# The low part of each weight chunk by a DMA that adds the raw chunk to its negated high part

## The chip, the cores and the metric

The kernel runs on one core of a Trainium2 chip. The metric is the device time of one execution in microseconds, as the median of the runs shown. TensorE is called PE, VectorE DVE, ScalarE ACT, GpSimd POOL and SyncE SP, as in the profile.

## What is computed

Two stacked blocks on a sequence of 512 tokens of width 1024. The first has two layers of dilated attention, an mLSTM, two gated projections and an MLP; the second has one layer with a state-space scan, top-k attention, a pooling mixer, three gated branches and a gated MLP. Almost all arithmetic is in the matrix products of the activations with float32 weights:

```python
def hybrid_layer(x, cos, sin, ...):
    h = rms_norm(x, norm_mix_w)
    z = h @ w_in + b_in
    ...
    mixed = ga * (ya @ w_proj_att) + gb * (yb @ w_proj_mlstm)
    x = x + mixed @ w_out
    h2 = rms_norm(x, norm_mlp_w)
    x = x + jnp.square(jax.nn.relu(h2 @ w_ff1)) @ w_ff2

def _layer(h, ...):
    proj = xn @ w_in
    ...
    merged = g[:, :, 0] * (y_ssd @ w_up_ssd) + g[:, :, 1] * (y_att @ w_up_attn) + g[:, :, 2] * (y_pool @ w_up_pool)
    h = h + merged @ w_out
    a_part, b_part = jnp.split(hn @ w_ffn_in, 2, axis=-1)
    return h + (jax.nn.silu(a_part) * b_part) @ w_ffn_out
```

## The kernel before, in words

**Three products for one.** PE multiplies in a float32 type with fewer mantissa bits (F32R). So each operand is split into a high part, which is the value rounded to that type, and a low part, the value minus its high part. A product of weights and activations is then high by high, high by low and low by high. In `lin` these are lines 280, 281 and 282: 280 and 281 read the high weights `wh`, and 282 reads the low weights `wl`. In `lin_tok` (319 to 321) the roles of the operands are exchanged.

**Chunks.** The weights come in chunks of 128 partitions by 1024 float32, 512 KB each, laid out on the host in the order of use. `chunk` (line 219) makes one ready. SP loads the raw chunk into `wr` (line 231). ACT copies it into `wh`, which rounds it (line 250). Then the low part `wl` is the raw chunk minus `wh`: on DVE (line 256), or in a fixed share of the chunks of some phases on POOL (line 254; the table `SHARE` sets the share). The first two chunks are made in pieces at lines 247 and 248, and the last few, with `keep`, go through `split`. `wr`, `wh` and `wl` have three buffers each, so a chunk's buffers come free when PE has done with the chunk three before it.

**The use of a chunk.** A chunk of a product over 1024 inputs holds one tile of 128 output columns and gives PE 24 matmuls. `lin_cols` (line 286) uses chunks one at a time, except for the first `lead` tiles of a call. With `lead` 2 the first two tiles are run together, each k of the one beside the same k of the other, so that both chunks must be there at nearly the same moment. I call two such chunks a pair, and a chunk that runs alone a single. By the table `LEAD` and the calls with `lead=2` there are, besides the pair that opens the program, 10 pairs in the first layer, 11 in the second (qk 1, gb 4, the output projection 1, ff1 1, ff2 4) and 25 in the second block (the gates of the branches 12, the state-space up-projection 4, the rest 9): 46 in all.

**Background work.** Attention, mLSTM, scan, indexer and pooling are generators that are advanced while the matrix products run (`tick`). All engines work their queues in order. A scheduler sets the order in each queue at build time, from its own estimates.

**The rotary embedding.** `ev_qk` (line 639) evacuates one of the eight query and key tiles, and its `turn` (lines 652 to 654) puts three operations on POOL. In the first layer these wait for `self.sin` (line 600).

```python
            h = self.wp.tile([P, CHUNK], F32R, name=self.name("wh"), tag="wh")
            nc.scalar.activation(h[:, :n], src, AF.Copy)
            nc.vector.tensor_tensor(lo[:, :n], src, h[:, :n].bitcast(F32), ALU.subtract)
```

Of the kernel before, what the change touches and what calls it, by code (L numbers as in the profile page):

```python
# [10 lines left out]
F32 = mybir.dt.float32  # L11
F32R = mybir.dt.float32r
I32 = mybir.dt.int32
AF = mybir.ActivationFunctionType
ALU = mybir.AluOpType
# [135 lines left out]
class Build:  # L151
# [67 lines left out]
    def chunk(self, key, l, rows, cs, keep=False):  # L219

        nc = self.nc
        kt, m = len(rows) // P, len(cs)
        i = self.nchunk
        self.nchunk += 1
        self.recipes.append((key, l, rows, cs))
        n = kt * m
        if i < 2:
            raw = self.raw[i]
        else:
            raw = self.wp.tile([P, CHUNK], F32, name=self.name("wr"), tag="wr")  # L230
            nc.sync.dma_start(raw[:, :n], self.dram["w"][i, :, :n])
        src = raw[:, :n]
        if keep:
            out = [], []
            for k in range(0, kt, 4):
                c = src[:, k * m : min(k + 4, kt) * m]
                for o, part in zip(out, self.split(c, n=c.shape[-1])):
                    o.extend(part[:, x * m : x * m + m] for x in range(min(4, kt - k)))
            return out
        h = self.wp.tile([P, CHUNK], F32R, name=self.name("wh"), tag="wh")  # L240
        lo = self.wp.tile([P, CHUNK], F32R, name=self.name("wl"), tag="wl")
        if i < 2:
            for a, b in FIRST:
                with ExitStack() as order:
                    for x in self.lead if a else ():
                        order.enter_context(self.tc.issue_after(x.ins))
                    nc.scalar.activation(h[:, a:b], src[:, a:b], AF.Copy)
                    nc.vector.tensor_tensor(lo[:, a:b], src[:, a:b], h[:, a:b].bitcast(F32), ALU.subtract)
            return tuple(x[:, :n].rearrange("p (k m) -> p k m", k=kt) for x in (h, lo))
        nc.scalar.activation(h[:, :n], src, AF.Copy)  # L250
        self.share += SHARE[self.phase]
        if self.share >= 1.0:
            self.share -= 1.0
            nc.gpsimd.tensor_tensor(lo[:, :n], src, h[:, :n].bitcast(F32), ALU.subtract)  # L254
        else:
            nc.vector.tensor_tensor(lo[:, :n], src, h[:, :n].bitcast(F32), ALU.subtract)  # L256
        v = lambda x: x[:, :n].rearrange("p (k m) -> p k m", k=kt)
        return v(h), v(lo)

# [1335 lines left out]
```

## Time and profile before

| | us |
|---|---|
| median of 3 runs | 2476.59 (2476.35 to 2478.15) |
| the profiled execution's own time | 2479.92 |
| its span, first to last instruction | 2478.1 |
| PE busy | 2442.3 (99%) |
| DVE busy | 1457.4 (59%) |
| ACT busy | 1005.0 (41%) |
| POOL busy | 438.7 (18%) |

The profiled execution is 3.3 us above the median. A matmul's duration in the trace overlaps the next one's, so the pace of PE is read from the distance of their starts. A wait is put down to the engine that the profile names as its releaser.

### The profile page before, as it was taken

Reading aid. Unit: us, or ns where it says so; the run is one execution under the profiler, and the core shown is the slowest. Engines: PE = TensorE matmul, PEld = TensorE weight load, DVE = VectorE, ACT = ScalarE, POOL = GpSimd, SP = SyncE. Lnnn points to the kernel's source line nnn. Section 1 sums busy time; section 2 is a strip of 40 time slices with the busy share of each in tenths; the row PEclk is TensorE's granted clock in tenths of the full one; section 3 lists DMA queues with packets and bytes.
Section 4 is the critical chain, followed back from the end, with each engine's and each line's share of the span. In section 5 each row is a group of like instructions: output and inputs, shape, how many; then the busy total and the mean of one; then the engine's idle time right before and its main releaser. Section 6 shows DMA issues by size and latency. Waiting matters only on the chain. (4 is left out here: it accounts for less than half of the span.)

```text
span 2478.1 us, 28176 instructions
## 1 busy us (share of the span) xinstructions
PE 2442.3 (99%) x10892; PEld 1950.7 (79%) x10892; DVE 1457.4 (59%) x2428; ACT 1005.0 (41%) x1483; POOL 438.7 (18%) x348
## 2 busy tenths in 40 slices
PE   9999999999999999999999999999999999999998
PEld 8777788888888877778888887777777778888887
DVE  7776655433447577655433446866898755434344
ACT  5567533332234377533332324344324633322222
POOL 4520010000311530011000120343332200101010
PEclk9999999999999999999999999999999999999999
DMA  4221223332223322223233332221222223332332
GB/s 160 90 79 54 69 85 95 102 94 94 94 94 94 98 65 77 68 77 102 86 102 96 94 99 86 77 85 52 80 84 70 77 77 94 102 94 92 96 91 71
DMA packets 63045, 216.46 MB, mean 87 GB/s; under 512 B 7232, under 2 KB 10304, under 8 KB 62912
## 3 DMA queue, kind: packets, MB, share of 16 engines
q1 hardware_dynamic: 60480, 212.14, 27.6%
q8 instruction: 85, 1.39, 0.2%
q10 hardware_dynamic: 2112, 1.48, 0.2%
q0 software_dynamic: 320, 1.05, 0.2%
q14 instruction: 48, 0.39, 0.0%
HBM read 212.55 MB, written 2.10 MB: 87 GB/s over the span
## 5 line engine op out<-in xcount | busy, mean ns | idle before, releaser
L280 PE MATMUL pb<-h,wh 128*128 128x512 f32 x2976 | 1199.8, 403 | 0.5 <-DVE tok L671 0.5
L282 PE MATMUL pb<-h,wl 128*128 128x512 f32 x2976 | 1180.8, 397 | 6.0 <-DVE wl L256 5.2
L281 PE MATMUL pb<-l,wh 128*128 128x512 f32 x2976 | 1180.5, 397 | 0.0
L250 ACT ACTIVATE wh<-wr 128x1024 fp32r<-128x1024 f32 (+1 forms) x393 | 410.6, 1054 | 959.9 <-PE pb L281 665.0
L282 PEld LDWEIGHTS pb<-h,wl 128*128 128x128 f32 x2976 | 562.9, 189 | 139.5 <-DVE wl L256 8.6
L280 PEld LDWEIGHTS pb<-h,wh 128*128 128x128 f32 x2976 | 563.0, 189 | 134.6 <-issue 8.2
L281 PEld LDWEIGHTS pb<-l,wh 128*128 128x128 f32 x2976 | 562.9, 189 | 130.0 <-issue 5.1
L256 DVE TENSOR_TENSOR wl<-wr,wh 128x1024 fp32r<-128x1024 f32 (+1 forms) x366 | 481.5, 1319 | 272.8 <-ACT wh L250 270.8
L254 POOL TENSOR_TENSOR wl<-wr,wh 128x1024 fp32r<-128x1024 f32 x27 | 67.7, 2506 | 403.2 <-ACT wh L250 362.3
L822 POOL TENSOR_TENSOR y<-y,rbc 128x512 f32<-128x512 f32 x16 | 24.7, 1542 | 561.3 <-DVE y L820 561.3
L1211 DVE TENSOR_TENSOR f<-pb,rbc 128x512 f32<-128x512 f32 x44 | 30.4, 691 | 123.9 <-PE pb L282 123.9
L1215 POOL TENSOR_TENSOR f<-f,fs 128x512 f32<-128x512 f32 x22 | 38.3, 1742 | 347.6 <-ACT fs L1214 347.6
L265 ACT ACTIVATE h<-f 128x512 fp32r<-128x512 f32 x86 | 54.4, 632 | 109.2 <-DVE f L808 88.1
L830 DVE TENSOR_TENSOR x<-x,pb 128x512 f32<-128x512 f32 x40 | 27.5, 688 | 99.3 <-PE pb L282 99.2
L266 DVE TENSOR_TENSOR l<-f,h 128x512 fp32r<-128x512 f32 x86 | 59.4, 690 | 44.8 <-ACT h L265 44.8
L525 DVE SCALAR_TENSOR_TENSOR cv<-cz,par,cv 128x512 f32<-128x512 f32 x84 | 73.0, 869 | 7.1 <-ACT cv L523 5.7
L820 DVE TENSOR_TENSOR y<-y,pb 128x512 f32<-128x512 f32 x32 | 22.0, 688 | 92.1 <-PE pb L282 92.1
L453 ACT ACTIVATE s<-s,ng 128x128 f32<-128x128 f32 (+3 forms) x96 | 53.4, 557 | 39.2 <-DVE ng L452 37.7
L319 PE MATMUL pb<-wh,h 128*128 128x512 f32 x128 | 51.0, 399 | 0.0
L320 PE MATMUL pb<-wh,l 128*128 128x512 f32 x128 | 50.7, 396 | 0.0
L735 DVE TENSOR_TENSOR gate<-pb,rbc 128x512 f32<-128x512 f32 x40 | 27.3, 687 | 39.4 <-PE pb L282 39.3
L321 PE MATMUL pb<-wl,h 128*128 128x512 f32 x128 | 50.4, 396 | 0.0
(396 smaller groups left out, 2365.5 us busy)
## 6 DMA issues: line engine op xcount, KB each, us to landing
wr<-in_w_dram SPq DMA_DIRECT2D x381, 512.0 KB, 3.6
wr<-in_w_dram SPq DMA_DIRECT2D x16, 448.0 KB, 3.3
x<-in_x_dram SPq DMA_DIRECT2D x8, 256.0 KB, 5.7
out_dram<-o SPq DMA_DIRECT2D x8, 128.0 KB, 2.4
out_dram<-o ACTq DMA_DIRECT2D x8, 128.0 KB, 2.5
wr<-in_w_dram SPq DMA_DIRECT2D x2, 384.0 KB, 5.4
bb<-in_bav_dram POOLq DMA_DIRECT2D x2, 256.0 KB, 3.9
bb<-in_bmv_dram POOLq DMA_DIRECT2D x2, 256.0 KB, 3.5
```

The lines of the kernel that those rows point to most:

```text
L250: nc.scalar.activation(h[:, :n], src, AF.Copy)
L254: nc.gpsimd.tensor_tensor(lo[:, :n], src, h[:, :n].bitcast(F32), ALU.subtract)
L256: nc.vector.tensor_tensor(lo[:, :n], src, h[:, :n].bitcast(F32), ALU.subtract)
L265: nc.scalar.activation(h[:, :n], src, AF.Copy)
L266: nc.vector.tensor_tensor(lo[:, :n], src, h[:, :n].bitcast(F32), ALU.subtract)
L280: mm(ps[:m, :], a, xh, start=k == 0, stop=False)
L281: mm(ps[:m, :], a, xl, start=False, stop=False)
L282: mm(ps[:m, :], b, xh, start=False, stop=k == n - 1)
L319: mm(ps[b], ah, wh[:, kk, :], start=k == 0, stop=False)
L320: mm(ps[b], al, wh[:, kk, :], start=False, stop=False)
L453: nc.scalar.activation(s[:, :n], s[:, :n], AF.Exp, bias=ng, scale=-1.0, accum_out=ls)
L525: nc.vector.scalar_tensor_tensor(a, z[:, 1 + j : 1 + j + T], w[:, j : j + 1], a, ALU.mult, ALU.add)
```

## The change

In the branch for chunks whose low part DVE made, two instructions take the place of the subtraction. ACT writes the raw chunk once more, negated, into `wl`; the output type rounds it, so this is the negated high part. Then POOL issues a DMA that reads the raw chunk a second time from DRAM and adds it onto `wl` in place. The branch for POOL's own subtractions stays.

```diff
         if self.share >= 1.0:
             self.share -= 1.0
             nc.gpsimd.tensor_tensor(lo[:, :n], src, h[:, :n].bitcast(F32), ALU.subtract)
         else:
-            nc.vector.tensor_tensor(lo[:, :n], src, h[:, :n].bitcast(F32), ALU.subtract)
+            nc.scalar.activation(lo[:, :n], src, AF.Copy, scale=-1.0)
+            nc.gpsimd.dma_start(lo[:, :n], self.dram["w"][i, :, :n], accum_op=ALU.add)
```

The scheduler orders every queue anew; lines below 256 have numbers one higher in the changed kernel. Three places matter for what follows.

The first is ACT's queue in the first layer, where a pair of chunks for `gb` is made while the single chunk before it runs. Before, `wh_2996` and `wh_3003` are the pair:

```order
L265 ACTIVATE h_2876<-m_638_2873 128x512
L250 ACTIVATE wh_2996<-wr_2994 128x1024
L250 ACTIVATE wh_3003<-wr_3001 128x1024
L736 ACTIVATE gate_2942<-gate_2942,par_130 128x512
L736 ACTIVATE gate_2945<-gate_2945,par_130 128x512
L265 ACTIVATE h_2971<-m_656_2968 128x512
```

Now the same pair is 3036 and 3044:

```order
L266 ACTIVATE h_2914<-m_638_2911 128x512
L250 ACTIVATE wh_3036<-wr_3034 128x1024
L256 ACTIVATE wl_3037<-wr_3034 128x1024
L737 ACTIVATE gate_2982<-gate_2982,par_130 128x512
L737 ACTIVATE gate_2985<-gate_2985,par_130 128x512
L250 ACTIVATE wh_3044<-wr_3042 128x1024
L256 ACTIVATE wl_3045<-wr_3042 128x1024
```

The two negated copies are new, and the second chunk's high part now stands behind the first chunk's negated copy and two gates.

The second is PE's queue where that pair is used (`pb_3000` and `pb_3007` before, `pb_3041` and `pb_3049` now, are the two output tiles). Before:

```order
L282 MATMUL pb_2955<-h_2762,wl_2951 128x512
L280 MATMUL pb_3000<-h_149,wh_2996 128x512
L281 MATMUL pb_3000<-l_150,wh_2996 128x512
L282 MATMUL pb_3000<-h_149,wl_2997 128x512
L280 MATMUL pb_3007<-h_149,wh_3003 128x512
L281 MATMUL pb_3007<-l_150,wh_3003 128x512
L282 MATMUL pb_3007<-h_149,wl_3004 128x512
L280 MATMUL pb_3000<-h_155,wh_2996 128x512
```

Now:

```order
L281 MATMUL pb_3041<-h_149,wh_3036 128x512
L282 MATMUL pb_3041<-l_150,wh_3036 128x512
L283 MATMUL pb_3041<-h_149,wl_3037 128x512
L281 MATMUL pb_3049<-h_149,wh_3044 128x512
L282 MATMUL pb_3049<-l_150,wh_3044 128x512
L281 MATMUL pb_3041<-h_155,wh_3036 128x512
L282 MATMUL pb_3041<-l_156,wh_3036 128x512
L283 MATMUL pb_3041<-h_155,wl_3037 128x512
L281 MATMUL pb_3041<-h_161,wh_3036 128x512
L282 MATMUL pb_3041<-l_162,wh_3036 128x512
L283 MATMUL pb_3041<-h_161,wl_3037 128x512
L283 MATMUL pb_3049<-h_149,wl_3045 128x512
```

The first low part is still needed at the third matmul of the pair, the second at the twelfth and not at the sixth.

The third is POOL's queue near the start, at the rotary embedding of the first layer (`rr` and `qk` are the tiles of `turn`). Before:

```order
L381 TENSOR_TENSOR acc_153<-acc_153,sq_202 128x512
L652 TENSOR_TENSOR rr_317<-rr_317,sin_324 128x512
L652 TENSOR_TENSOR rr_322<-rr_322,sin_324 128x512
L653 TENSOR_TENSOR qk_277<-qk_277,cos_325 128x512
L653 TENSOR_TENSOR qk_319<-qk_319,cos_325 128x512
L654 TENSOR_TENSOR qk_277<-qk_277,rr_317 128x512
L654 TENSOR_TENSOR qk_319<-qk_319,rr_322 128x512
L652 TENSOR_TENSOR rr_368<-rr_368,sin_324 128x512
L653 TENSOR_TENSOR qk_365<-qk_365,cos_325 128x512
L654 TENSOR_TENSOR qk_365<-qk_365,rr_368 128x512
```

Now (the DMAs of the chunks at index 5 and 6, `wl_457` and `wl_497`):

```order
L257 DMA wl_457<-in_w_dram 128x1024
L653 TENSOR_TENSOR rr_317<-rr_317,sin_324 128x512
L653 TENSOR_TENSOR rr_322<-rr_322,sin_324 128x512
L654 TENSOR_TENSOR qk_277<-qk_277,cos_325 128x512
L654 TENSOR_TENSOR qk_319<-qk_319,cos_325 128x512
L655 TENSOR_TENSOR qk_277<-qk_277,rr_317 128x512
L655 TENSOR_TENSOR qk_319<-qk_319,rr_322 128x512
L653 TENSOR_TENSOR rr_369<-rr_369,sin_324 128x512
L654 TENSOR_TENSOR qk_366<-qk_366,cos_325 128x512
L257 DMA wl_497<-in_w_dram 128x1024
L655 TENSOR_TENSOR qk_366<-qk_366,rr_369 128x512
```

The DMA of the chunk at index 6 now stands behind eight of these operations, and the later ones behind three or four each. POOL's queue has 366 such DMAs in all.

## Rows read from the trace of the kernel before

**Rows 1.** The page: span, then busy time, share of the span and instructions.
```profile
span 2478.1 us, 28176 instructions
PE 2442.3 (99%) x10892; PEld 1950.7 (79%) x10892; DVE 1457.4 (59%) x2428; ACT 1005.0 (41%) x1483; POOL 438.7 (18%) x348
```
**Rows 2.** Groups of instructions: busy us, mean ns of one, idle before and its releaser.
```profile
L250 ACT ACTIVATE wh<-wr 128x1024 fp32r<-128x1024 f32 (+1 forms) x393 | 410.6, 1054 | 959.9 <-PE pb L281 665.0
L256 DVE TENSOR_TENSOR wl<-wr,wh 128x1024 fp32r<-128x1024 f32 (+1 forms) x366 | 481.5, 1319 | 272.8 <-ACT wh L250 270.8
L254 POOL TENSOR_TENSOR wl<-wr,wh 128x1024 fp32r<-128x1024 f32 x27 | 67.7, 2506 | 403.2 <-ACT wh L250 362.3
```
**Rows 3.** Waits of PE and its weight loads: us in total, times, longest.
```profile
PE PT L464 <- DVE ng L452: 6.0, 3, 3.6
PE pb L282 <- DVE wl L256: 5.2, 4, 2.7
PEld pb L282 <- DVE wl L256: 8.6, 7, 3.1
```
**Rows 4.** ACT in order of time, singles of the MLP: start, duration.
```profile
499.30 1.06 ACT L250 ACTIVATE wh<-wr 128x1024 fp32r<-128x1024 f32 x1 [4.04 <-PE pb L281]
500.26 0.57 ACT L818 COPY y<-pb 128x512 f32<-128x512 f32 x1
```
**Rows 5.** PE in order of time: first use of that chunk's low part.
```profile
510.94 0.40 PE L282 MATMUL pb<-h,wl 128*128 128x512 f32 x1
```
**Rows 6.** ACT and DVE in order of time, while a pair is made ready.
```profile
335.81 2.01 ACT L250 ACTIVATE wh<-wr 128x1024 fp32r<-128x1024 f32 x2 [3.29 <-PE pb L281]
337.72 1.32 ACT L736 ACTIVATE gate<-gate,par 128x512 f32<-128x512 f32 x2
335.99 1.39 DVE L735 TENSOR_TENSOR gate<-pb,rbc 128x512 f32<-128x512 f32 x2 [2.75 <-PE pb L282]
```
**Rows 7.** PE in order of time: that pair's first matmul and first low parts.
```profile
342.07 0.39 PE L280 MATMUL pb<-h,wh 128*128 128x512 f32 x1
342.53 0.39 PE L282 MATMUL pb<-h,wl 128*128 128x512 f32 x1
343.23 0.40 PE L282 MATMUL pb<-h,wl 128*128 128x512 f32 x1
```
**Rows 8.** The page: DMA queue (packets, MB, share), then issues (KB, us to landing).
```profile
q1 hardware_dynamic: 60480, 212.14, 27.6%
wr<-in_w_dram SPq DMA_DIRECT2D x381, 512.0 KB, 3.6
bb<-in_bav_dram POOLq DMA_DIRECT2D x2, 256.0 KB, 3.9
bb<-in_bmv_dram POOLq DMA_DIRECT2D x2, 256.0 KB, 3.5
```
**Rows 9.** Groups of POOL: a DMA's issue, us and mean ns.
```profile
L667 POOL DMA_DIRECT2D bb<-in_bav_dram x2 | 1.3, 660 | 0.0
```
**Rows 10.** POOL in order of time, from the first rotary operation on.
```profile
42.29 2.67 POOL L652 TENSOR_TENSOR rr<-rr,sin 128x512 f32<-128x512 f32 x2 [20.75 <-DVE sin L600]
44.90 3.55 POOL L653 TENSOR_TENSOR qk<-qk,cos 128x512 f32<-128x512 f32 x2
48.42 3.53 POOL L654 TENSOR_TENSOR qk<-qk,rr 128x512 f32<-128x512 f32 x2
51.91 1.30 POOL L652 TENSOR_TENSOR rr<-rr,sin 128x512 f32<-128x512 f32 x1
53.16 1.31 POOL L653 TENSOR_TENSOR qk<-qk,cos 128x512 f32<-128x512 f32 x1
```
**Rows 11.** DVE in order of time: evacuation of the eighth query and key tile.
```profile
58.95 0.69 DVE L641 TENSOR_TENSOR qk<-pb,rbc 128x512 f32<-128x512 f32 x1 [2.73 <-PE pb L282]
```
**Rows 12.** PE after its longest wait; busy by stretch (PE's and PEclk matter).
```profile
120.87 0.90 PE L464 MATMUL PT<-first,s 128*128 128x128 f32 x3 [3.58 <-DVE ng L452]
120.00:125.00 5.00, 4.13 (x14) 3.56 (x15) 3.80 (x9) 2.80 (x6) 0.00 (x0) 0.50 0.02 6
```

## The prediction, made before the changed kernel ran

> **What bounds the kernel now.** I read the page's busy times first: PE is busy 2442.3 of 2478.1 us [rows 1], so only 36 us of its time are idle, and an edit that frees DVE (1457.4 us busy) cannot give more than that. Then the groups of instructions: 366 low parts are made by DVE, 1319 ns each, 27 by POOL, and ACT waits 665 us for PE before its high parts [rows 2]. So the chunks are made ahead of PE, as early as a buffer comes free. The waits say the same: PE stands for a low part only 5.2 us in 4 waits, its weight loads 8.6 us in 7 [rows 3]; the two overlap. What decides is therefore the slack: the time from a finished high part to PE's first use of the low part.
>
> For a single the high part ends at 499.30 + 1.06 = 500.36 [rows 4] and the low part is first used at 510.94 [rows 5]: 10.6 us. For a pair the high parts end at 336.87 and 337.82 [rows 6] and the low parts are first used at 342.53 and 343.23 [rows 7]: 5.7 and 5.4 us, because only one single runs between the release of the buffers and the pair. PE's matmuls start 0.23 us apart [rows 7], a chunk of 24 takes 5.57 us.
>
> **What the change does to a chunk.** Removed: 366 DVE subtractions, 481.5 us [rows 2]. PE is the bound, so this gives at most what PE still waits for DVE; apart from the low parts its longest entry is 6.0 us [rows 3]. I take 5 us off, with 0 and 14 as ends. The 27 subtractions on POOL stay.
>
> Added on ACT: 366 negated copies of the same shape as the high part, 1.05 us each [rows 2], 386 us. ACT goes from 41% to 56% and is not the bound, but the copy stands between the high part and the DMA, and in front of the next high part. Added on POOL: 366 DMA issues of about 0.66 us [rows 9], 242 us, which would bring it from 18% to 28%; each waits in order for ACT's copy and behind POOL's other work, and whatever POOL has queued behind it waits too.
>
> **The new DMA's time, L, from issue to landing.** No row shows an accumulating DMA. The raw loads took 27.6% of 16 engines for 212.14 MB [rows 8]: 0.276 x 2478.1 / 212.14 x 0.524 = 1.69 us of all 16 engines for a 512 KB chunk. POOL's own loads of 256 KB land after 3.5 and 3.9 us [rows 8]; less 0.85 us of data that leaves about 2.85 us of fixed time. The new DMA must read the chunk from DRAM and also what it adds to, so I count its data twice: 2.85 + 3.38 = 6.2 us. The raw load for the chunk three later is released by the same ACT copy and runs beside it, for up to 1.69 us more. I take L = 6.5. Ends: 3.6, a plain raw load from SP's queue [rows 8], and 2.85 + 3.38 + 1.69 = 7.9. The doubled price is nearest to the rows of POOL's loads, which is why I stay there.
>
> For the accumulate itself only a page has a price: the Trainium skill (Collectives: The Full Stack, section "The bandwidth ceiling: the fold count and why AG ≠ RS ≠ AR") has an adding transfer at half a copy's rate, because it makes two source reads on one ring. By it the data would take 3.4 us, the value above; no run here shows it yet.
>
> **Singles.** High part ready at 500.36, perhaps a 0.57 us evacuation [rows 4], copy 1.05, then L: landing at 508.5 for L = 6.5 and 509.9 for 7.9, before 510.94. Nothing is lost. The cover that hides the DMA is two whole chunks of PE work; an L beyond 8.9 would break it.
>
> **Pairs.** ACT's queue as it stands now, with the times of [rows 6]: first high part until 336.87, its copy until 337.9, two gates (1.32 us) until 339.2, second high part until 340.2, its copy until 341.3. So the DMAs are issued at 338.0 and 341.4. PE reaches the pair at 342.07 [rows 7]; the first low part is needed at 342.53, the second, by the new order of PE (the twelfth matmul), at 342.07 + 11 x 0.23 = 344.6. The first lands at 338.0 + L, 2.0 us late for L = 6.5; the second at 341.4 + L = 347.9, 3.3 us late, of which 2.0 are already passed. So a pair loses L - 3.2 us in all: 3.3 for L = 6.5, 0.4 for 3.6, 4.7 for 7.9. The program text has 46 pairs: **+152 us**, with ends of 18 and 216. I let this one pair stand for all. Where PE already waits for low parts (11 waits) [rows 3] there is no slack to lose first; I add 1 us for each, **+10**.
>
> **POOL's queue at the start.** The DMA for the chunk at index 6 stands behind eight rotary operations. These begin at 42.29, when the sine is ready, and the eighth ends at 54.5 [rows 10]. So the chunk lands at 61.0. When is it needed? The eighth tile is evacuated at 58.95 right after PE ends it [rows 11], so the seventh began 2 x 5.57 earlier, at 47.8, and needs its low part at 48.2. **+13** (9.9 to 14.2). The later ones have three or four such operations each, 4 to 5 us, and keep about PE's pace.
>
> A rule speaks to this place: two operations of one kind took 3.55 us there, and one a little later 1.31 [rows 10]. The Trainium skill (SBUF — State Buffer, section "Who interferes with whom") says that a DVE instruction with two SBUF inputs contends with GpSimd's reads; by it, the removed subtractions would free POOL, the eight would take 10.4 us and not 12.2, and the 13 would be 11. The same section says that a copy or `tensor_scalar` on DVE in its two-port mode keeps GpSimd from writing descriptors, which would make L longer; DVE's instruction there is a `tensor_tensor` [rows 6], so the sum stays.
>
> **Sum.** 152 + 10 + 13 - 5 = +170 on the profiled 2479.9, 2650; the median of the runs is 3.3 us lower: **2647 us**, +6.9%. With the low ends, 18 + 0 + 10 - 14, it is about 2490, with the high ones, 216 + 10 + 14, about 2717.
>
> **Rivals.**
>
> *The DMA engines become the bound.* Raw load and accumulate together take 1.69 x 3 = 5.1 us of all 16 engines per 5.57 us chunk by my price, so little is free. If the accumulate moves at a third of a copy's rate, it is 1.69 x 4 = 6.76 us, 1.2 us more than PE needs: 366 x 1.2 = 440 us, some 2920 us. For it: nothing in [rows 8] shows what an addition costs, and the margin is 9%. Against: the doubled count is what the bytes ask for. It decides from a factor of 2.3 on. 22%.
>
> *Nearly hidden.* With L near 3.6, pairs lose 0.4 us and the total is 2481 to 2500. For it: the 512 KB loads do land in 3.6 us. Against: half the size takes 3.5 to 3.9 us from POOL's queue [rows 8]. 7%; 5% more for an end within 0.2% of before (some 5 us, about what a measurement of this kernel can tell from no change).
>
> *Faster.* If L is below 3.2 us, no pair waits, and what DVE is relieved of shows. POOL, without DVE's subtractions beside it, may do its eight rotary operations at 1.30 us each [rows 10], 10.4 us; then the chunk there lands at 42.3 + 10.4 + 3.2 = 55.9, 7.7 us late, and against it stand up to 14 us of waits on DVE that go: 6 us less, 2470 us. It decides at L = 3.2; all of [rows 8] lie above. 4%.
>
> *PE's clock falls after the new gaps.* After the 3.58 us wait the granted clock was 0.50 from 120 to 125 us, which is 1.2 of 2.4 GHz [rows 12]. PE did nothing just before. If the pairs' gaps of 2 to 3 us do the same, each costs about 2.5 us more, up to 46 x 2.5 = 115 us, some 2760 us; part of it would be given back, since a slower PE needs the second low part later. 10%.
>
> **How the numbers follow.** The forecast, pairs waiting 1 to 5 us each (2500 to 2740), has 52%; the clock 10%, the engines as the bound 22%, nearly hidden 7%, no change 5%, faster 4%. So faster 0.04, same 0.05, slower 0.91. The range goes from 2490, the low ends, to 2950, just past the case at a third of the rate; what stays out is some 11% below (the faster case, the unchanged one, and a little of the nearly hidden one) and some 9% above, where the accumulate is slower still.
>
> **What would show it.** In the profile after: the accumulating DMA's landing time (about 6.5 us), its share of the engines (about twice the raw loads' per byte), PE waiting for `wl` at the L282 that is now L283, 2 to 3 us at pairs and not at singles, and a gap of some 13 us near 48 to 61 us. DVE's busy time falls by some 480 us, ACT's rises by 386. If PE waits at singles as well, or the engines are over 90% busy, the first rival holds; if the landing is under 4 us, the second. If PE's clock stays at 1.0 through the pairs, the fourth is out. I am wrong if PE has no waits for low parts and the time is still far from before, or if the waits come from ACT's copies and not from the landing.

## The result, and the profile after

The changed kernel takes 2817.9 us (median of 4 runs, 2814.9 to 2824.2) against 2476.7 (4 runs) for the kernel before on the same chip: 1.138 times as long, 95% interval 1.136 to 1.140, or +341 us. The forecast was +170, so the sign held, but the forecast had only half of the loss.

The page of the changed kernel, span and busy times, then the two DMA queues that matter (packets, MB, share of 16 engines):

```profile
span 2812.8 us, 28945 instructions
...
PE 2552.8 (91%) x10892; PEld 2014.0 (72%) x10892; DVE 1015.4 (36%) x2062; ACT 1335.8 (47%) x1849; POOL 693.6 (25%) x714
...
q0 software_dynamic: 53024, 192.18, 37.7%
q1 hardware_dynamic: 60480, 212.14, 26.5%
```

Against [rows 1] the span is 334.7 us longer. PE does the same 10,892 matmuls, but is busy 110.5 us longer (2552.8 less 2442.3) and idle 224.2 us longer (260.0 against 35.8). These are the two halves of the loss, and they add up to it. DVE has 442 us less to do, ACT 331 more, POOL 255 more; none of the three is near the span.

The idle half has one name. Waits of PE and of its weight loads (us in total, times, longest), and the groups of the low part (busy, mean ns of one, idle before and its releaser):

```profile
PEld pb L283 <- DMA wl<-in_w_dram: 259.1, 79, 6.6
PE pb L283 <- DMA wl<-in_w_dram: 224.7, 71, 6.2
...
PE pb L322 <- DMA wl<-in_w_dram: 10.4, 3, 4.9
```

```profile
L283 PE MATMUL pb<-h,wl 128*128 128x512 f32 x2976 | 1226.8, 413 | 225.5 <-DMA wl<-in_w_dram 224.7
...
L257 POOL DMA_DIRECT2D wl<-in_w_dram x366 | 318.4, 871 | 1733.9 <-ACT wl L256 1605.5
...
L256 ACT ACTIVATE wl<-wr 128x1024 fp32r<-128x1024 f32 (+1 forms) x366 | 381.1, 1042 | 0.4 <-PE pb L283 0.3
```

PE stands 235.1 us for the landing of low parts, where before it stood 5.2 us for DVE [rows 3]. The DMA issues (KB, median us from issue to landing) say how long one takes:

```profile
wr<-in_w_dram SPq DMA_DIRECT2D x381, 512.0 KB, 5.0
wl<-in_w_dram POOLq DMA_DIRECT2D x354, 512.0 KB, 7.7
```

The adding DMA lands after 7.7 us, and the raw load beside it after 5.0 where it was 3.6 [rows 8]. Over the whole span the engines are not full: these two queues take 37.7% + 26.5% of their time. Per 512 KB chunk the adding DMA takes 0.377 x 2812.8 / 192.18 x 0.524 = 2.89 us of all 16 engines.

Where PE waits is read from one stretch of the MLP. PE in order of time, a pair's first low part at 528.58 and, 20 us later, another wait; then ACT between the two, and POOL's issue:

```profile
528.58 0.50 PE L283 MATMUL pb<-h,wl 128*128 128x512 f32 x1 [2.42 <-DMA wl<-in_w_dram]
...
549.13 0.79 PE L283 MATMUL pb<-h,wl 128*128 128x512 f32 x1 [4.25 <-DMA wl<-in_w_dram]
```

```profile
538.27 1.06 ACT L250 ACTIVATE wh<-wr 128x1024 fp32r<-128x1024 f32 x1 [10.42 <-issue]
539.24 1.06 ACT L819 COPY y<-pb 128x512 f32<-128x512 f32 x2
540.18 1.07 ACT L256 ACTIVATE wl<-wr 128x1024 fp32r<-128x1024 f32 x1
```

```profile
541.55 0.86 POOL L257 DMA_DIRECT2D wl<-in_w_dram  x1 [13.07 <-ACT wl L256]
```

The wait at 549.13 belongs to a single, not to a pair. A pair's matmuls are interleaved, so it gives both its buffers back at its end. The first chunk behind it was made ready while the pair ran; the second gets its buffer only now, its high part ends at 539.33 and PE wants its low part at 549.13 - 4.25 = 544.88, 5.6 us later. That is the pair's own slack (5.4 and 5.7 us in the kernel before [rows 6, 7]), not the 10.6 us of the single that I had read.

The busy half is the clock. Busy time by stretch (PE, PEld, DVE, ACT, POOL with their counts, granted clock, DMA share, GB/s), behind the shorter of the two waits, inside the longer (two rows), behind it, and after that:

```profile
528.00:534.00 6.00, 5.42 (x23) 4.45 (x24) 0.57 (x1) 0.00 (x0) 0.48 (x1) 1.00 0.79 174
545.00:547.00 2.00, 0.00 (x0) 0.00 (x0) 0.00 (x0) 1.76 (x3) 0.00 (x0) 1.00 0.98 188
547.00:549.00 2.00, 0.00 (x0) 0.00 (x0) 0.00 (x0) 0.00 (x0) 0.86 (x1) 0.70 1.04 293
549.00:554.00 5.00, 4.87 (x12) 3.81 (x13) 0.00 (x0) 0.00 (x0) 0.00 (x0) 0.50 1.05 271
554.00:560.00 6.00, 6.00 (x26) 4.90 (x25) 0.00 (x0) 2.49 (x3) 0.36 (x1) 0.95 0.22 46
```

After the 2.42 us the clock stays at 1.00 (2.4 GHz); after the 4.25 us it is 0.50 (1.2 GHz) for five microseconds, in which PE does 12 matmuls where 6 us of nearly full clock hold 26. It falls while PE does nothing: the row before has a mean of 0.70.

The same rows show what the mean over the span hides. Inside the longer wait the DMA engines are full (0.98 and 1.04): three adding DMAs and three raw loads are under way behind this pair, and the adding ones land after 7.5, 9.6 and 9.7 us.

### The profile page after: what moved, and what is told of

It is laid out like the page before. It is cut to its first block, busy times and chain, and to the rows that moved or that the text cites. A ratio compares the mean times of both kernels' runs of the same rounds, so it can differ in the third digit from the quotient of the medians.

```text
span 2812.8 us, 28945 instructions
## 1 busy us (share of the span) xinstructions
PE 2552.8 (91%) x10892; PEld 2014.0 (72%) x10892; DVE 1015.4 (36%) x2062; ACT 1335.8 (47%) x1849; POOL 693.6 (25%) x714
## 3 DMA queue, kind: packets, MB, share of 16 engines
q0 software_dynamic: 53024, 192.18, 37.7%
q1 hardware_dynamic: 60480, 212.14, 26.5%
## 5 line engine op out<-in xcount | busy, mean ns | idle before, releaser
L283 PE MATMUL pb<-h,wl 128*128 128x512 f32 x2976 | 1226.8, 413 | 225.5 <-DMA wl<-in_w_dram 224.7
L281 PE MATMUL pb<-h,wh 128*128 128x512 f32 x2976 | 1231.8, 414 | 0.0
L282 PE MATMUL pb<-l,wh 128*128 128x512 f32 x2976 | 1212.1, 407 | 1.9 <-DVE l L270 1.9
L283 PEld LDWEIGHTS pb<-h,wl 128*128 128x128 f32 x2976 | 583.6, 196 | 396.4 <-DMA wl<-in_w_dram 259.1
L257 POOL DMA_DIRECT2D wl<-in_w_dram x366 | 318.4, 871 | 1733.9 <-ACT wl L256 1605.5
L282 PEld LDWEIGHTS pb<-l,wh 128*128 128x128 f32 x2976 | 583.2, 196 | 142.1 <-issue 5.5
L281 PEld LDWEIGHTS pb<-h,wh 128*128 128x128 f32 x2976 | 585.2, 197 | 137.2 <-issue 7.0
L256 ACT ACTIVATE wl<-wr 128x1024 fp32r<-128x1024 f32 (+1 forms) x366 | 381.1, 1042 | 0.4 <-PE pb L283 0.3
L809 DVE TENSOR_TENSOR f<-f,pb 128x512 f32<-128x512 f32 x64 | 44.0, 687 | 328.8 <-ACT f L808 328.8
L322 PE MATMUL pb<-wl,h 128*128 128x512 f32 x128 | 51.6, 414 | 10.4 <-DMA wl<-in_w_dram 10.4
```

Source lines behind the costliest of these rows:

```text
L256: nc.scalar.activation(lo[:, :n], src, AF.Copy, scale=-1.0)
L257: nc.gpsimd.dma_start(lo[:, :n], self.dram["w"][i, :, :n], accum_op=ALU.add)
L281: mm(ps[:m, :], a, xh, start=k == 0, stop=False)
L282: mm(ps[:m, :], a, xl, start=False, stop=False)
L283: mm(ps[:m, :], b, xh, start=False, stop=k == n - 1)
```

## Experiments

The theory after this reading: PE waits for the landing wherever only one chunk of PE work covers it, at the pairs and at the second chunk behind a pair, and it pays part of each longer wait again by a half clock. Rivals: the load of the DMA engines slows everything; ACT's second pass over each chunk does it; GpSimd's queue is slow by itself. The first four kernels ran before I had seen the second chunk behind the pair; their expectations speak of pairs alone. "Before" is always the median of the kernel before on the same chip, 2478.7 us for these four.

**ACT's copy without the DMA.**

```diff
             nc.scalar.activation(lo[:, :n], src, AF.Copy, scale=-1.0)
-            nc.gpsimd.dma_start(lo[:, :n], self.dram["w"][i, :, :n], accum_op=ALU.add)
+            nc.vector.tensor_tensor(lo[:, :n], src, lo[:, :n].bitcast(F32), ALU.add)
```

> ScalarE's negated copy stays as it is, but VectorE and not the DMA adds the raw chunk to it. Theory (the DMA's landing is what PE waits for): the copies lie under PE's work, 2475 to 2490 us. Rival (ScalarE's second pass over each chunk delays the high parts and low parts by itself): most of the loss stays, 2650 us or more.

Measured: 2478.0 us, ratio 1.000 (0.999 to 1.001). ACT is busy 1337.1 us there, as in the changed kernel, and it costs nothing. The second pass over the chunk is out as a cause by itself.

**Pairs from VectorE, and the reverse.** A chunk of a pair is one that is requested with one tile per chunk while more than one tile is led (`per == 1 and j < min(lead, len(tiles))`). The second kernel has `elif not pair`.

```diff
...
+        elif pair:
+            nc.vector.tensor_tensor(lo[:, :n], src, h[:, :n].bitcast(F32), ALU.subtract)
         else:
             nc.scalar.activation(lo[:, :n], src, AF.Copy, scale=-1.0)
```

> The low parts of the pairs' chunks come from VectorE again, every other one by the adding DMA. Theory: the pairs' slack is too short for the DMA's landing (7.7 us), and nearly all waits are there; then the 235 us of waits and the some 120 us of half clock behind them go but for the few at single chunks and in the branch stage: 2480 to 2520 us. Rival, the DMA engines' load costs time everywhere: three quarters of the transfers stay, so about three quarters of the 341 us do, some 2730 us.

> The reverse: only the pairs' low parts come by the adding DMA, the others from VectorE. Theory (the pairs' slack): the loss stays nearly whole, 2720 to 2820 us; where the DMA engines are much less loaded the landing may shorten from 7.7 towards 6.5 us, which would take up to 46 x 1.2 = 55 us of waits off. Rival (the load of the engines): a quarter of the transfers, a quarter of the loss, some 2560 us.

Measured: pairs from VectorE 2590.6 us (+111.9, ratio 1.045, 1.044 to 1.047); pairs alone by DMA 2710.2 us (+231.5, ratio 1.094, 1.092 to 1.096). The two losses add up to 343, the whole change costs 341. By count, three quarters of the transfers (284 of 366) carry a third of the loss, so the engines' load does not set it; but the first result lies 70 us above what the theory of the pairs alone allowed, and between it and the rival. Busy times and the group of the low parts' matmuls (idle before, and its releaser, at the end), with all but the pairs by DMA:

```profile
PE 2478.3 (96%) x10892; PEld 1971.5 (76%) x10892; DVE 1106.8 (43%) x2144; ACT 1262.3 (49%) x1767; POOL 632.6 (24%) x632
...
L285 PE MATMUL pb<-h,wl 128*128 128x512 f32 x2976 | 1196.5, 402 | 76.6 <-DMA wl<-in_w_dram 71.5
```

With the pairs alone by DMA, and the landing of theirs:

```profile
PE 2517.7 (93%) x10892; PEld 1992.3 (74%) x10892; DVE 1364.5 (50%) x2346; ACT 1079.1 (40%) x1565; POOL 496.8 (18%) x430
...
L285 PE MATMUL pb<-h,wl 128*128 128x512 f32 x2976 | 1212.3, 408 | 161.7 <-DMA wl<-in_w_dram 161.0
...
wl<-in_w_dram POOLq DMA_DIRECT2D x80, 512.0 KB, 7.7
```

The landing's median is 7.7 us whether all 366, the 284 outside the pairs or these 82 come by the adding DMA, so it does not follow their number. Single landings run from 5.7 to 10.1 us here, so what is under way beside a DMA moves them, by how much was not separated. Pairs wait 161.0 us and lose 2517.7 - 2442.3 = 75.4 us of clock; the others wait 71.5 us (and 9.6 at the token-major sums) and lose 36.0. So about half of each wait is paid again. The waits at chunks of no pair sent me back to the stretch at 549 us shown above.

**Filling the pair's wait with work.**

```diff
+FILLS = 16
...
+        if len(tiles) == 2 and tiles[0][1] is not tiles[1][1]:
+            ps, (wh, wl), m0, m = tiles[0]
+            for _ in range(FILLS):
+                mm(ps[:m, :], wh[:, 0, m0 : m0 + m], xs[0][0], start=True, stop=True)
```

> Before each pair PE does 16 matmuls with the first chunk's high part that are thrown away (3.7 us at full clock), so that it works through most of the wait instead of standing still. Theory (the half clock behind each gap costs about as much again as half of the wait, some 120 us): the clock stays up, and the time falls although PE does more: 2690 to 2740 us. Rival (the time is the waits alone, whatever the clock): the extra matmuls lie in the wait and change nothing, 2810 to 2830 us, or lengthen it where a wait is shorter than 3.7 us.

Measured: 2889.7 us, ratio 1.166 (1.164 to 1.167): a miss for both. PE at one pair, in order of time (the 16 extra matmuls are at L282):

```profile
376.42 3.89 PE L282 MATMUL pb<-h,wh 128*128 128x512 f32 x16
380.15 0.39 PE L286 MATMUL pb<-h,wh 128*128 128x512 f32 x1
380.38 0.39 PE L287 MATMUL pb<-l,wh 128*128 128x512 f32 x1
380.61 0.39 PE L288 MATMUL pb<-h,wl 128*128 128x512 f32 x1
380.84 0.39 PE L286 MATMUL pb<-h,wh 128*128 128x512 f32 x1
381.08 0.40 PE L287 MATMUL pb<-l,wh 128*128 128x512 f32 x1
384.83 0.79 PE L288 MATMUL pb<-h,wl 128*128 128x512 f32 x1 [3.36 <-DMA wl<-in_w_dram]
```

The fill covers the first low part, which is there at 380.61. But in this kernel's order the second chunk's low part is the sixth matmul and not the twelfth, and its DMA was issued some 3.5 us after the first's: the wait is the second's now. PE still waits 167.9 us in all, and the 752 extra matmuls add 188.7 us. This run says nothing on the clock by itself; extra work in front of a pair is no remedy while the second landing is the later one.

**The second chunk behind a pair as well.** Added to the kernel with the pairs from VectorE; 20 more chunks move, 264 stay with the DMA.

```diff
+        self.since = 0 if pair else self.since + 1
...
-        elif pair:
+        elif pair or self.since == 2:
```

> As with the pairs' low parts on VectorE, and in addition that of the second chunk behind each pair (the low part that PE waits 4.25 us for at 549.13 us of the changed kernel's trace). Theory: a pair gives both its buffers back at its end, so the second chunk behind it has one single of PE work for cover, as the pair has; it is where the other third of the loss lies. Its 72 us of waits and 36 us of half clock go, and what is left are the few waits of the start and the branch stage: 2480 to 2510 us. Rival (the landing is too slow for any chunk now and then, by what else the DMA engines carry): the waits move to other chunks, 2550 to 2590 us.

Measured: 2502.9 us against 2479.3, ratio 1.010 (1.008 to 1.011). These 20 chunks take 88 us off 2590.6; 264 chunks by DMA are left and cost 24 us. Busy times and the low parts' group:

```profile
PE 2452.2 (98%) x10892; PEld 1953.7 (78%) x10892; DVE 1130.5 (45%) x2164; ACT 1243.8 (50%) x1747; POOL 618.3 (25%) x612
...
L286 PE MATMUL pb<-h,wl 128*128 128x512 f32 x2976 | 1183.9, 398 | 17.3 <-DMA wl<-in_w_dram 11.5
...
wl<-in_w_dram POOLq DMA_DIRECT2D x255, 512.0 KB, 7.6
```

The busy time is back within 10 us of the 2442.3 before: the clock's half goes when the waits go. The landing is still 7.6 us.

**High parts first.** Instead of sparing the DMA the tight chunks, the low parts are needed later. In a pair alone (the condition of the fill above), then for every chunk, then the same order in the kernel before:

```diff
+HIGH_FIRST = True
...
+        if HIGH_FIRST:
+            steps = [(k, t, r) for k in range(n) for t in tiles for r in "hl"]
+            steps += [(k, t, "w") for t in tiles for k in range(n)]
+            for i, (k, (ps, (wh, wl), m0, m), r) in enumerate(steps):
+                a = (wl if r == "w" else wh)[:, k, m0 : m0 + m]
+                mm(ps[:m, :], a, xs[k][r == "l"], start=k == 0 and r == "h", stop=k == n - 1 and r == "w")
+                if i % 3 == 2:
+                    self.tick()
+            return
```

> The change as it is, but PE does a pair's 32 products with the high parts first (7.4 us) and its 16 with the low parts after them. Theory: the pair's waits (some 160 us and 75 us of half clock) go, since the low parts are needed 3.2 to 7 us later; the waits at the second chunk behind a pair stay: 2570 to 2610 us. Rival (PE must wait for the landings wherever they come, so a wait avoided at the pair comes back behind it): 2700 us or more.

> The same order, high parts first, for every chunk: a single's first low part is needed 3.7 us later, a pair's 7.4 us. Theory: waits of up to 3.7 us at the second chunk behind a pair go, longer ones shrink by that (4.25 to 0.6 us): 2480 to 2530 us. Rival (the later end of the low products holds the buffers longer, and the chunks behind come later by as much): 2560 us or more.

> The kernel before with the same order, high parts first. It has 5.2 us of waits for low parts, so the order can give it some 5 to 10 us at most: 2465 to 2478 us, or no difference; if the order by itself costs something, this shows how much.

Measured against 2479.3: pairs only 2555.0 us, ratio 1.031 (1.029 to 1.032), some 15 us below the theory's range and far from its rival; every chunk 2492.5 us, ratio 1.005 (1.004 to 1.006); the kernel before in that order 2482.4 us, ratio 1.0014 (1.0006 to 1.0023), so the order by itself gives nothing. With every chunk high parts first, the page's busy times, queue, the low parts' group and the landing:

```profile
PE 2443.6 (98%) x10892; PEld 1947.5 (78%) x10892; DVE 1015.8 (41%) x2062; ACT 1371.7 (55%) x1849; POOL 695.1 (28%) x714
...
q0 software_dynamic: 53024, 192.18, 42.9%
...
L284 PE MATMUL pb<-h,wl 128*128 128x512 f32 x2976 | 772.6, 398 | 2.9 <-DMA wl<-in_w_dram 2.9
...
wl<-in_w_dram POOLq DMA_DIRECT2D x354, 512.0 KB, 7.8
```

And of all its groups, that of the token-major sum (`lin_tok`):

```profile
L332 PE MATMUL pb<-wl,h 128*128 128x512 f32 x128 | 52.5, 420 | 13.2 <-DMA wl<-in_w_dram 13.2
```

All 366 adding DMAs are there, land after 7.8 us, and the engines carry more per us than in the changed kernel; yet PE waits 2.9 us at the chunks, and its busy time is that of before. So the transfers are affordable, and the 341 us were a matter of when PE asks for them. The rest is the token-major sum, 13.2 us.

**The same, and the token-major sum's low parts from VectorE.** `lin_tok` asks for its chunks with `pair=True`. It makes the token-major products in the two layers of the first block; the expectation is wrong to place them in the branch stage.

> High parts first for every chunk, and the low parts of the token-major products (the branch stage's four-chunk sums, where PE still stands 13.2 us in 4 waits) from VectorE; all others by the adding DMA. Theory: these 13 us are the rest of the loss, so the time is that of the kernel before, 2474 to 2484 us; DVE's 400 us less cannot make it faster, since PE's busy time alone is some 2440 us. Rival (something else still costs): 2488 to 2495 us as with high parts first alone.

Measured: 2470.0 us against 2477.7, ratio 0.9964 (0.9951 to 0.9976): 8 us faster than the kernel before, and 12 below that kernel in the same order. I had written that relief of DVE could give nothing, and that was wrong by these few microseconds:

```profile
span 2467.5 us, 28943 instructions
...
PE 2439.9 (99%) x10892; PEld 1944.3 (79%) x10892; DVE 1040.7 (42%) x2077; ACT 1358.4 (55%) x1834; POOL 687.3 (28%) x699
...
L286 PE MATMUL pb<-h,wl 128*128 128x512 f32 x2976 | 773.8, 399 | 3.9 <-DMA wl<-in_w_dram 3.8
```

PE is idle for 27.6 us, 8 less than in [rows 1]; of it the wait for DVE's low parts was 5.2 [rows 3]. Which of DVE's other waits make up the rest was not tried. This version is 0.4% below the kernel before.

**The DMA without its addition.**

```diff
-            nc.gpsimd.dma_start(lo[:, :n], self.dram["w"][i, :, :n], accum_op=ALU.add)
+            nc.gpsimd.dma_start(lo[:, :n], self.dram["w"][i, :, :n])
```

> The same DMA on the same queue without the addition; the low part is then the raw chunk, the subtraction is left out. Theory (the addition, which reads twice what it writes, makes most of the landing): its packets take about half as long, the landing is 4.5 to 5.5 us, and a pair and the second chunk behind it lose about 2 to 3 us less each: 2520 to 2640 us. Rival (the queue of GpSimd, with its descriptors written by GpSimd, is slow by itself): 7 us or more, and 2780 to 2830 us.

This kernel leaves out the subtraction. Measured: 2548.4 us against 2477.7, ratio 1.028 (1.026 to 1.030).

```profile
PE 2457.6 (97%) x10892; PEld 1945.0 (77%) x10892; DVE 1016.5 (40%) x2062; ACT 1335.1 (53%) x1849; POOL 578.9 (23%) x714
...
q0 software_dynamic: 53024, 192.18, 22.0%
...
L283 PE MATMUL pb<-h,wl 128*128 128x512 f32 x2976 | 1188.2, 400 | 57.8 <-DMA wl<-in_w_dram 56.9
...
L257 POOL DMA_DIRECT2D wl<-in_w_dram x366 | 201.3, 550 | 1596.2 <-ACT wl L256 1534.5
...
wl<-in_w_dram POOLq DMA_DIRECT2D x354, 512.0 KB, 4.6
```

The plain DMA lands after 4.6 us and takes 0.220 x 2539.7 / 192.18 x 0.524 = 1.52 us of the engines. The addition makes it 7.7 and 2.89: 3.1 us more of landing, 1.9 times the engines' time, and 871 ns instead of 550 of issue on POOL. The queue by itself is not what is slow. And the waits are shorter here (56.9 us in 46 waits, 1.2 us each) and are followed by a busy time only 15.3 us above [rows 1], a quarter of the waits and not a half.

**Two DMAs for each chunk.**

```diff
+            for a in range(0, n, 512):
+                nc.gpsimd.dma_start(lo[:, a : min(a + 512, n)], self.dram["w"][i, :, a : min(a + 512, n)], accum_op=ALU.add)
```

> Each adding DMA is issued as two, one for each half of the chunk's products (256 KB each). If the halves share the engines in order, the first lands some 1.5 us (half of 2.9 us of data) earlier; PE needs the second half only 2.8 us after the first. Theory: waits shorten by about 1 us each, 2700 to 2790 us. Rival (the fixed part of the landing and twice the issues decide; the first half lands no earlier, or the second is issued 0.9 us later and lands later): 2810 us or more.

Measured: 2704.0 us against 2477.7, ratio 1.091 (1.089 to 1.093): a third of the loss is gone. A half lands after 6.4 us (720 issues of 256 KB), 1.3 us earlier than a whole chunk; PE waits 143.2 us at L284, and POOL pays 658.4 us for 732 issues, which it has.

## Why the prediction had the sign and half of the size

The forecast was right on the pairs: they wait for the landing, because one chunk of PE work does not cover it, and none of the other engines is at its limit over the span. It failed in two terms that it put at nothing, some of the singles and the clock. Its sum was 152 + 10 + 13 - 5 = 170. What each term became, in the span's 334.7 us:

| term | forecast | measured |
| --- | --- | --- |
| waits at pairs | 152 | 161.0 (pairs alone by DMA) |
| where PE already waited for DVE | 10 | not told apart, in the row of the singles |
| token-major sums | not in the sum | 10.4 (waits at L322) |
| start, behind the rotary operations | 13 | 4.4 |
| singles | 0 | about 59 (224.7 - 161.0 - 4.4) |
| PE's other idle time | -5 | -10.9 (224.2 - 235.1) |
| PE's clock | 0 | 110.5 |

**The step that failed first is "Singles ... Nothing is lost".** I read one single, the one at 499.30 [rows 4, 5], and let it stand for all. The second chunk behind a pair, five chunks earlier, shows another slack in the same kernel. ACT of the kernel before, that chunk's high part and what stands behind it, then PE's first use of its low part:

```profile
476.34 1.06 ACT L250 ACTIVATE wh<-wr 128x1024 fp32r<-128x1024 f32 x1 [6.88 <-PE pb L281]
477.31 1.05 ACT L818 COPY y<-pb 128x512 f32<-128x512 f32 x2
```

```profile
483.06 0.39 PE L282 MATMUL pb<-h,wl 128*128 128x512 f32 x1
```

From 477.40 to 483.06 are 5.7 us, and two evacuations stand between this high part and its negated copy. The 10.6 us hold only from where the buffers come free one by one. With 20 such chunks on VectorE the time fell by 88 us, clock included.

**The second is the clock, left out of the sum.** I had its row [rows 12] and its price, up to 115 us, and made it a rival at 10%. But a forecast of 46 waits of about 3.3 us should have carried its consequence: the one row that I had behind a wait of that size showed 0.50. Measured, 110.5 us more busy time for the same matmuls. It is not another way in which it could go but the second half of the same one: with the pairs alone, 75.4 us behind 161.0 of waits, with the others alone 36.0 behind 71.5.

**L was mis-sized, 6.5 for 7.7 us, and the pairs' term hardly felt it.** By L - 3.2 a pair would lose 4.5 us and all 207; the pairs alone waited 161.0. So the slack of 3.2 us, read at one pair, was about 1 us short for the mean, and the two errors offset each other: that this term came out within 6% is luck. My high end of 7.9 was the better estimate of L. The count of the data was right (1.9 times measured, 2 taken). What I had too low is the rest of the landing, 7.7 - 2.89 = 4.8 us against 4.6 - 1.52 = 3.1 of the plain DMA; why it is longer stays open. The raw loads beside it went from 3.6 to 5.0 us as well.

The Trainium skill (Collectives: The Full Stack, "The bandwidth ceiling: the fold count and why AG ≠ RS ≠ AR") has the adding transfers of a ring between cores at half the rate of the copying ones. As an estimate by it, the plain 1.52 us would become 3.04; the trace has 2.89, so it agrees within 5%, here for a load from DRAM into the on-chip buffer.

**Where PE already waited.** The 11 waits behind the +10 were 4 of PE and 7 of its weight loads, and these overlap, so the count was too high. They lie in the second block, between 1700 and 1990 us. The 10.4 us at L322 belong to another place, `lin_tok` in the first block, where PE did not stand before at all; that the two numbers agree is chance. With the pairs from VectorE, PE waits for a landing once in the branch stage, 3.5 us.

**The start.** POOL's queue did stop the DMA of the chunk at index 6, but for 4.4 us and not 13. POOL of the changed kernel, and PE's wait:

```profile
43.77 2.56 POOL L654 TENSOR_TENSOR qk<-qk,cos 128x512 f32<-128x512 f32 x2
46.29 2.55 POOL L655 TENSOR_TENSOR qk<-qk,rr 128x512 f32<-128x512 f32 x2
...
51.29 0.80 POOL L257 DMA_DIRECT2D wl<-in_w_dram  x1
```

```profile
56.92 0.79 PE L283 MATMUL pb<-h,wl 128*128 128x512 f32 x1 [4.44 <-DMA wl<-in_w_dram]
```

POOL's pairs of operations take 2.56 us where they took 3.55 [rows 10], and the first begins at 41.13 instead of 42.29, so the DMA goes out at 51.29, not 54.5, and lands 5.6 us later. In the kernel with ACT's copy alone DVE still does an operation with two inputs for each chunk, there at 46.85 (1.24 us) and 51.42. The pair of POOL operations beside the first takes as long as before, the pair between the two does not:

```profile
45.73 3.53 POOL L654 TENSOR_TENSOR qk<-qk,cos 128x512 f32<-128x512 f32 x2
49.22 2.55 POOL L655 TENSOR_TENSOR qk<-qk,rr 128x512 f32<-128x512 f32 x2
```

The Trainium skill (SBUF — State Buffer, "Who interferes with whom") says that a DVE instruction with two SBUF inputs contends with a POOL instruction that reads SBUF. The traces agree: 3.55 and 3.53 us with such an instruction on DVE beside them, 2.56 and 2.55 without. PE also came there later than I had worked out, at 52.5 and not 48.2.

**Rivals.** The engines as the bound, 22%: out, the adding DMA costs 1.9 and not 2.3 times a plain one, and with high parts first the same transfers fit into a span of 2485 us. My sign for this rival, that PE waits at singles as well, was badly chosen: PE did wait at singles, but at those behind a pair, and for the pairs' reason. Nearly hidden, 7%, and unchanged, 5%: out, L is 7.7. Faster, 4%: not for this change, but a gain of its kind, 8 us, shows in the last version of the high parts first, where the landing is covered. The clock, 10%: true, beside the forecast.

## What to carry to other kernels

When a producer is replaced by a slower one that is started earlier, the question is the shortest slack among all consumers, so read it for each position around a group that releases its buffers together: the members of the group, and the chunk as far behind it as the buffers reach. Where PE is the bound and the new producer makes it wait for microseconds, add the clock to the wait in the sum, from a row behind such a wait. And a landing that is too late can be met by the consumer's order: here the same transfers cost 341 us or about 13, depending on whether the low parts are asked for first or last.

## What the runs showed of the hardware

- An adding DMA of 512 KB from DRAM lands after 7.7 us in the median, the same DMA without the addition after 4.6. It takes 2.89 us of all 16 engines against 1.52, and its issue on POOL 871 ns against 550.
- The raw loads beside it, on another queue, go from 3.6 to 5.0 us, though the engines are busy for 64% of the span (they are full in bursts, such as the one at 545 to 549 us); beside the plain DMA they stay at 3.6.
- The same 10,892 matmuls keep PE busy for 2439.0 us (ACT's copy alone) to 2552.8 us (the changed kernel). The surplus over the 2442.3 of before is about half of the waits for landings where these are some 3 us in the mean, a quarter where they are 1.2 us; behind a wait of 4.25 us the granted clock was 0.50, behind one of 2.42 us 1.00.
